# One encoder step: input and output projection in 7 Strassen products instead of 8, attention's data kept in device memory

## The chip, the cores and the metric

The kernel runs on one core of a Trainium2 chip. The metric is the device time of one execution in microseconds (us). A core has five engines with a program each: PE (TensorE, matrix products), DVE (VectorE), ACT (ScalarE), POOL (GpSimd) and SP, which here only issues transfers. They work side by side and wait for one another through semaphores. Operands lie in the on-chip buffer SBUF; PE writes its results into the accumulators PSUM, from which DVE and ACT take them in this kernel.

## The reference

One step of a hybrid encoder layer on 1056 tokens (a prompt of 1024 and a sample of 32), width 1024, everything in 32-bit floats:

```python
p = rmsnorm(x, g) @ w_in                       # 1024 -> 7424 columns
q, k, v, ga, bb, cc, hh, gb, xq, gx, mg = split(p)
attn  = window_attention(q, k, v, sink, alibi) # 8 heads, chunks of 64, 128 back
conv  = conv3(cc * hh, w, b)                   # 3 taps, each channel by itself
xattn = cross_attention(xq, mk, mv)            # 4 heads, 256 memory tokens, mk, mv = rmsnorm(mem) @ w
ya = (attn * silu(ga)) @ w_pa                  # 512 -> 1024
yb = (bb * conv * silu(gb)) @ w_pb
yx = (xattn * silu(gx)) @ w_px
sa, sb, sx = split(sigmoid(mg))
y = rmsnorm(x + (sa * ya + sb * yb + sx * yx) @ w_out, final_g)
```

The kernel also returns the new keys and values and the convolution's state.

## The kernel before

Activations lie with channels on the 128 partitions and tokens along the free dimension. Precision is kept by splitting each operand into a rounded high part and a rest (hi and lo, both in the type fp32r), and each product is three matmuls, hi·hi, hi·lo and lo·hi (`mm3`, L115 to L118). Tokens go in 3 chunks of 352.

x is loaded unnormalised, multiplied by the norm's gain and split once into `xhi` and `xlo` (`split_scaled`, L141). The input projection has 58 tiles of 128 output channels. Each tile and chunk is 8 pieces of the inner dimension times 3 matmuls of 352 columns into one PSUM bank, which DVE then multiplies by R, the reciprocal root mean square of each token (`scaled`, L285). Weights come as 172 pieces of 128x512 in the order of use: a load into `wraw`, a cast into `whi` on ACT (L102) and a subtraction into `wlo` on POOL (L103, the first 19 on DVE). They are made two or three pieces ahead of their use.

The order of the work is written out by hand: memory keys and values, k, v, q, then window attention and cross attention cut into steps that stand between the tiles of the other projections, the 24 tiles `mg` of the merge's gates in the middle, then the branch projections `y_tile` (matmuls of 352 columns) with the merge `z` (DVE L350 and POOL L662). `z` is split into `zhi` and `zlo` (L880). The output projection `wo` takes two forms: six blocks of 128 tokens with 512 columns, and the other 288 tokens with channels on the partitions (`wf`), turned by PE. One DVE instruction each adds the residual (L935), ACT sums the squares, POOL takes the power −0.5 and the result is scaled and stored block by block.

## Time and profile before

| | |
|---|---|
| three runs | 1050.56, 1051.35 and 1051.8 us, median 1051.35 us |
| the profiled execution | 1050.6 us span, as long as the fastest run |
| PE busy | 1033.7 us (98%) |
| DVE, ACT, POOL busy | 394.2, 338.7, 372.1 us |
| moved | 68.90 MB, 66 GB/s in the mean |

A busy time counts an engine's instructions with their overlaps taken out. For matmuls, which are pipelined, the spacing of the starts is the cost of one, and its own duration is longer. The chain of work that ended last says which engine the end waited for.

### The profile page before, as it was taken

Reading aid. Unit: us, or ns where it says so; the run is one execution under the profiler, and the core shown is the slowest. Engines: PE = TensorE matmul, PEld = TensorE weight load, DVE = VectorE, ACT = ScalarE, POOL = GpSimd, SP = SyncE. Lnnn points to the kernel's source line nnn. Section 1 sums busy time; section 2 is a strip of 40 time slices with the busy share of each in tenths; the row PEclk is TensorE's granted clock in tenths of the full one; section 3 lists DMA queues with packets and bytes.
Section 4 is the critical chain, followed back from the end, with each engine's and each line's share of the span. In section 5 each row is a group of like instructions: output and inputs, shape, how many; then the busy total and the mean of one; then the engine's idle time right before and its main releaser. Section 6 shows DMA issues by size and latency. Waiting matters only on the chain.

```text
span 1050.6 us, 16279 instructions
## 1 busy us (share of the span) xinstructions
PE 1033.7 (98%) x6531; PEld 1002.4 (95%) x6531; DVE 394.2 (38%) x747; ACT 338.7 (32%) x786; POOL 372.1 (35%) x353
## 2 busy tenths in 40 slices
PE   8999999999999999999999999999999999989997
PEld 7899999999999999999999999999999999988886
DVE  5736777773211244454111112222322111154122
ACT  7754555552121233344112111211212221233132
POOL 0353334241221232232333354434433453466210
PEclk9999999999999999999999999999999999999999
DMA  8861101011111111112111111111211221115112
GB/s 288 300 196 33 36 21 41 21 31 41 51 41 51 45 38 31 42 31 71 45 47 51 41 41 51 51 41 41 59 43 41 71 71 41 51 33 184 49 67 100
DMA packets 34827, 68.90 MB, mean 66 GB/s; under 512 B 4416, under 2 KB 5824, under 8 KB 34752
## 3 DMA queue, kind: packets, MB, share of 16 engines
q1 hardware_dynamic: 34752, 67.87, 20.5%
q8 instruction: 51, 0.84, 0.3%
q14 instruction: 24, 0.20, 0.1%
HBM read 62.31 MB, written 5.55 MB: 65 GB/s over the span
## 4 chain that ended last, share of the span: by engine, by line
PE 87%; DVE 7%; ACT 3%; issue 2%; DMA 1%; SPq 0%; DVEq 0%; POOLq 0%; POOL 0%; ACTq 0%
PE mg L116 8%; PE mg L117 8%; PE mg L118 8%; PE y L116 4%; PE y L117 4%; PE y L118 4%; PE wo L116 2%; PE wo L118 2%; PE wo L117 2%; PE gx L118 1%; PE gx L117 1%; PE xq L117 1%; PE xq L116 1%; PE xq L118 1%; PE gb L118 1%
## 5 line engine op out<-in xcount | busy, mean ns | idle before, releaser
L103 POOL TENSOR_TENSOR wlo<-wraw,whi 128x512 fp32r<-128x512 f32 x141 | 183.3, 1301 | 363.3 <-ACT whi L102 363.2
L102 ACT CAST whi<-wraw 128x512 fp32r<-128x512 f32 x160 | 99.0, 621 | 277.0 <-PE y L117 96.0
L116 PE MATMUL mg<-xhi,whi 128*128 128x352 f32 x576 | 186.6, 324 | 0.0
L117 PE MATMUL mg<-xlo,whi 128*128 128x352 f32 x576 | 185.8, 323 | 0.0
L118 PE MATMUL mg<-xhi,wlo 128*128 128x352 f32 x576 | 185.8, 323 | 0.0
L285 DVE TENSOR_TENSOR mg<-mg,R 128x352 f32<-128x352 f32 x72 | 38.3, 532 | 199.9 <-PE mg L118 199.7
L116 PEld LDWEIGHTS mg<-xhi,whi 128*128 128x128 f32 x576 | 108.2, 188 | 0.5
L117 PEld LDWEIGHTS mg<-xlo,whi 128*128 128x128 f32 x576 | 108.2, 188 | 0.0
L118 PEld LDWEIGHTS mg<-xhi,wlo 128*128 128x128 f32 x576 | 108.2, 188 | 0.0
L347 ACT ACTIVATE sg<-mg 128x352 f32<-128x352 f32 x51 | 23.7, 466 | 105.2 <-DVE mg L285 103.6
L662 POOL TENSOR_TENSOR z<-z,sg 128x352 f32<-128x352 f32 x42 | 39.7, 946 | 22.0 <-DVE sg L350 22.0
L350 DVE SCALAR_TENSOR_TENSOR sg<-sg,y 128x352 f32<-128x352 f32 x48 | 25.0, 520 | 59.2 <-PE y L118 46.6
L427 ACT ACTIVATE sw<-sw,mxw 128x256 f32<-128x256 f32 x64 | 31.8, 498 | 39.5 <-DVE mxw L444 39.4
L431 POOL TENSOR_TENSOR sw<-sw,rdw 128x1024 f32<-128x1024 f32 x16 | 30.3, 1896 | 29.7 <-DVE rdw L452 19.2
L116 PE MATMUL q<-xhi,whi 128*128 128x352 f32 x96 | 32.1, 334 | 0.0
L116 PE MATMUL y<-xqhi,whi 128*128 128x352 f32 x96 | 31.8, 331 | 0.0
L116 PE MATMUL ga<-xhi,whi 128*128 128x352 f32 x96 | 31.8, 331 | 0.0
L117 PE MATMUL y<-xqlo,whi 128*128 128x352 f32 x96 | 31.6, 329 | 0.0
L118 PE MATMUL y<-xqhi,wlo 128*128 128x352 f32 x96 | 31.5, 328 | 0.0
L116 PE MATMUL xq<-xhi,whi 128*128 128x352 f32 x96 | 31.2, 325 | 0.0
L116 PE MATMUL gx<-xhi,whi 128*128 128x352 f32 x96 | 31.2, 325 | 0.0
L117 PE MATMUL ga<-xlo,whi 128*128 128x352 f32 x96 | 31.1, 324 | 0.0
(354 smaller groups left out, 2770.8 us busy)
## 6 DMA issues: line engine op xcount, KB each, us to landing
wraw<-in_wst SPq DMA_DIRECT2D x172, 256.0 KB, 2.6
xsx<-in_x_prompt SPq DMA_DIRECT2D x8, 512.0 KB, 6.2
out_y_p<-y SPq DMA_DIRECT2D x7, 512.0 KB, 2.6
xp<-in_xT SPq DMA_DIRECT2D x6, 528.0 KB, 4.5
res<-in_x_prompt SPq DMA_DIRECT2D x8, 256.0 KB, 4.2
xp<-in_xT SPq DMA_DIRECT2D x3, 352.0 KB, 5.0
xsm<-in_mem_prompt SPq DMA_DIRECT2D x2, 512.0 KB, 5.2
x1z<-in_x_prompt SPq DMA_DIRECT2D x3, 256.0 KB, 6.9
```

Source lines behind the costliest of these rows:

```text
L102: act.copy(hi, raws[i])
L103: (eng or pool).tensor_tensor(out=lo, in0=raws[i], in1=hi.bitcast(F32), op=ALU.subtract)
L116: pe.matmul(out, lh, rh, start=first, stop=False)
L117: pe.matmul(out, lh, rl, start=False, stop=False)
L118: pe.matmul(out, ll, rh, start=False, stop=last)
L285: dve.tensor_tensor(out=ps, in0=ps, in1=R[:, ts], op=ALU.mult)
L347: act.activation(out, x, AF.Tanh, scale=0.5)
L350: dve.scalar_tensor_tensor(out=out, in0=t, scalar=1.0, in1=x, op0=ALU.add, op1=ALU.mult)
L427: act.activation(dst[:n, j, :w], src[:n, j, :w], AF.Exp, bias=nmx[:n, j:j + 1], scale=scale, accum_out=den[:n, j:j + 1])
L431: pool.tensor_tensor(out=s2v[:n, :cols, :w], in0=s2v[:n, :cols, :w], in1=rd[:n, :cols].unsqueeze(2).broadcast_to([n, cols, w]), op=ALU.mult)
L662: (pool if tail is None else dve).tensor_tensor(out=z, in0=z, in1=s[:, ts], op=ALU.add)
```

## The change

The tokens go in two halves c, of 528 tokens each, and each half again in two quarters of 264. For a pair of output tiles, the two halves of the inner dimension, the two output tiles and the two quarters of tokens make a 2x2 by 2x2 block product, which the Strassen-Winograd scheme does with 7 block products and sums of blocks (`group`). Both halves c are done with the same weights in the input projection, so that a group has 7 x 2 x 4 x 3 = 168 matmuls of 264 columns, where two tiles had 144 of 352.

For this x is normalised before it is used (`x_norm`), and the seven sums of its blocks are made and split (`x_combine`, 28 tiles). The weights need four sums of pieces on DVE per group (`Weights.comb`), and seven splits instead of four, with the subtraction on POOL unless a list names DVE. The seven results are put together with one copy or activation on ACT, a second one (`c11`), and five additions on DVE, each of a PSUM tile and an SBUF tile.

Since the 28 operand tiles fill the SBUF, q, k, v, the gates, the keys and values of the memory and the outputs of the branches are stored to device memory (`move`) and loaded back in pieces. Attention is cut into 51 units of four steps each, which are spread evenly over the products of the groups from `xq` on. The memory's keys and values are computed without a split, in plain fp32 matmuls. The output projection is done for one half c after the other: four groups each, of 84 matmuls, and the weights are combined and split again for the second half. It has channels on the partitions, and the result is stored transposed.

```diff
-        def split_scaled(raw, g, hi, lo):
-            act.activation(hi, raw, AF.Copy, scale=g)
-            dve.scalar_tensor_tensor(out=lo, in0=raw, scalar=g, in1=hi.bitcast(F32), op0=ALU.mult, op1=ALU.subtract)
...
-        def scaled(ps, ts):
-            dve.tensor_tensor(out=ps, in0=ps, in1=R[:, ts], op=ALU.mult)
-        def proj_chunk(w, c, evac, nm):
-            ps = pp.tile([128, CH], F32, name=f"{nm}_{c}", tag="pp")
-            ts = slice(c * CH, (c + 1) * CH)
-            for k in range(8):
-                wh, wl = w[k // 4]
-                cs = slice((k % 4) * 128, (k % 4 + 1) * 128)
-                mm3(ps, wh[:, cs], wl[:, cs], xhi[:, k, ts], xlo[:, k, ts], k == 0, k == 7)
-            evac(c, ts, ps)
...
-        def wo_token_major(half, i, c0, n_cols, ps):
-            ts = slice(i * 128, (i + 1) * 128)
-            for k in range(8):
-                wh, wl = splits[n_stream + half * 8 + k]
-                cs = slice(c0, c0 + n_cols)
-                mm3(ps, zhi[:, k, ts], zlo[:, k, ts], wh[:, cs], wl[:, cs], k == 0, k == 7)
...
-        def add_square(r, ps, n, acc, nm):
-            dve.scalar_tensor_tensor(out=r, in0=ps, scalar=0.5, in1=r, op0=ALU.mult, op1=ALU.add)
-            jk = wk.tile([128, 512], F32, name=f"jk{nm}", tag="pth", bufs=2)
-            act.activation(jk[:n, :r.shape[1]], r, AF.Square, accum_out=acc)
...
+        def move(out, in_):
+            out, in_ = (x.bitcast(F32) if x.dtype == F32R else x for x in (out, in_))
+            sp.dma_start(out=out, in_=in_)
...
+        def w_pair(src, name, eng=None):
+            n = src.shape[1]
+            hi = sb.tile([128, n], F32R, name=f"wh{name}", tag="whi", bufs=4)
+            lo = sb.tile([128, n], F32R, name=f"wl{name}", tag="wlo", bufs=4)
+            act.copy(hi, src)
+            sub_lo(eng or pool, lo, src, hi)
+            return hi, lo
...
+            def comb(self, i, a, b, op):
+                s = sb.tile([128, 512], F32, name=f"S{i}_{self.nm}", tag="S", bufs=3)
+                dve.tensor_tensor(out=s, in0=a, in1=b, op=op)
+                return s
+            def make(self, j):
+                self.load()
+                a11, a21, a22, a12 = self.raws
+                if j == 0:
+                    src = a11
+                elif j == 1:
+                    self.s1 = self.comb(1, a21, a22, ALU.add)
+                    src = self.s2 = self.comb(2, self.s1, a11, ALU.subtract)
+                elif j == 2:
+                    src = a12
+                elif j == 3:
+                    src = self.s1
+                elif j == 4:
+                    src = self.comb(3, a11, a21, ALU.subtract)
+                elif j == 5:
+                    src = self.comb(4, a12, self.s2, ALU.subtract)
                 else:
+                    src = a22
+                return w_pair(src, f"{self.nm}_{j}", self.engs[j])
...
+        def product(ps, cs, j, w, first, last):
+            for i, c in enumerate(cs):
+                for k in range(4):
+                    kc = slice(k * 128, (k + 1) * 128)
+                    mm3(ps[:, i, :H], w[0][:, kc], w[1][:, kc], XA[c][j][0][k], XA[c][j][1][k],
+                        first and k == 0, last and k == 3, True)
...
+            def s0():
+                st["a"], st["b"] = out_tile(0), out_tile(1)
+                st["pa"] = acc("pa", one_)
+                product(st["pa"], cs, B11, pair(), True, True)
+                act.copy(quad(st["a"], 0, cs), pv(st["pa"], cs))
+            def s1():
+                p = acc("pb", 1 - one_)
+                product(p, cs, T2, pair(), True, True)
+                st["u2"] = half("u2", f"u2{nm}")
+                dve.tensor_tensor(out=flat(st["u2"], cs), in0=pv(p, cs), in1=quad(st["a"], 0, cs), op=ALU.add)
+            def s2():
+                product(st["pa"], cs, B21, pair(), False, True)
+                c11(quad(st["a"], 0, cs), pv(st["pa"], cs))
+            def s3():
+                st["pc"] = acc("pc", 1 - one_)
+                product(st["pc"], cs, T1, pair(), True, True)
+                dve.tensor_tensor(out=quad(st["b"], 1, cs), in0=pv(st["pc"], cs), in1=flat(st["u2"], cs), op=ALU.add)
+            def s4():
+                st["pd"] = acc("pd", one_)
+                product(st["pd"], cs, T3, pair(), True, True)
+                q = quad(st["b"], 1, cs)
+                dve.tensor_tensor(out=q, in0=pv(st["pd"], cs), in1=q, op=ALU.add)
+            def s5():
+                product(st["pc"], cs, B22, pair(), False, True)
+                dve.tensor_tensor(out=quad(st["a"], 1, cs), in0=pv(st["pc"], cs), in1=flat(st["u2"], cs), op=ALU.add)
+                done(0, st["a"])
+            def s6():
+                product(st["pd"], cs, T4, pair(), False, True)
+                dve.tensor_tensor(out=quad(st["b"], 0, cs), in0=pv(st["pd"], cs), in1=flat(st["u2"], cs), op=ALU.add)
+                done(1, st["b"])
...
+            move(out=dst(0), in_=hi)
+            move(out=dst(1), in_=lo)
...
+        def x_norm(c, R):
+            for k in range(8):
+                dve.scalar_tensor_tensor(out=xk(c, k), in0=xk(c, k), scalar=cst[:, C_G + k:C_G + k + 1], in1=R,
+                                         op0=ALU.mult, op1=ALU.mult)
...
+            def put(op, kk, src):
+                hi, lo = (t[:, kk * 528:(kk + 1) * 528].rearrange("p (k h) -> p k h", k=2) for t in op)
+                act.copy(hi, src)
+                sub_lo((dve, pool, dve, pool, pool)[n[0] % 5], lo, src, hi)
+                n[0] += 1
...
+            def comb(out, a, b):
+                dve.tensor_tensor(out=out, in0=a, in1=b, op=ALU.subtract)
...
+            for kk in range(2):
+                put(b11, kk, xb(c, 0, 0, kk))
+            for kk in range(2):
+                t, u = (x[:, 2 * kk:2 * kk + 2] for x in tt)
+                comb(t, xb(c, 0, 1, kk), xb(c, 0, 0, kk))
+                comb(u, xb(c, 1, 1, kk), t)
+                put(t2, kk, u)
+                put(t1, kk, t)
+                t1s.append(u)
+                if kk == 0:
+                    b21 = operand(c, B21)
+                put(b21, kk, xb(c, 1, 0, kk))
...
+        def mv_step(k, w):
+            if k == 0:
                 for m in range(2):
+                    mps[m] = bank2(f"mvp{m}")[:, 0]
+            for m in range(2):
+                pe.matmul(mps[m], mt(k)[:, m * 128:(m + 1) * 128], w, start=k == 0, stop=k == 7)
...
+        units = win + [WindowSample()] + [Cross(h, u) for h in range(4) for u in range(4)] + [CrossSample(0), CrossSample(1)]
+        events = sorted((k + d, k, what) for k in range(len(units))
+                        for d, what in ((0.0, "load"), (1.0, "scores"), (2.5, "turn"), (3.02, "out")))
+        steps = [st for g in G[n_first:] for st in g]
+        end = events[-1][0] + 1
+        for i, st in enumerate(steps):
+            st()
+            while events and events[0][0] * (len(steps) - 4) <= i * end:
+                _, k, what = events.pop(0)
+                getattr(units[k], what)()
...
+        def z_put(c, j, p, src):
+            hi, lo = ZO[c, j][0][p], ZO[c, j][1][p]
+            act.copy(hi, src)
+            zn[0] += 1
+            sub_lo((dve, pool)[zn[0] % 2], lo, src, hi)
...
+        def z_second(c, p):
+            (z0, z1), (w0, w1) = z_pair(c, p), z_pair(c, 2 + p)
+            dve.tensor_tensor(out=z0, in0=w1, in1=z0, op=ALU.subtract)
+            z_put(c, T2, p, z0)
+            z_put(c, B21, p, w0)
+            pool.tensor_tensor(out=z1, in0=w1, in1=z1, op=ALU.subtract)
+            z_put(c, T3, p, z1)
+            z_put(c, B22, p, w1)
+            dve.tensor_tensor(out=w0, in0=w0, in1=z0, op=ALU.subtract)
+            z_put(c, T4, p, w0)
...
+            def done(i, r):
+                g = f + i
+                x = half("gt", f"xres{c}_{g}", F32, 3)
+                move(out=x, in_=A["xT"][c, g // 2][:, (g % 2) * 528:(g % 2 + 1) * 528])
+                dve.scalar_tensor_tensor(out=r, in0=r, scalar=0.5, in1=x, op0=ALU.mult, op1=ALU.add)
+                s = s2_tile(f"rsq{c}_{g}")
+                act.activation(s, r, AF.Square)
+                if g:
+                    pool.tensor_tensor(out=s, in0=s, in1=RT[c, "acc"], op=ALU.add)
+                RT[c, "acc"] = s
...
+        def finish(c):
+            R = r_chunk([RT[c, "acc"]], f"o{c}")
+            for g in range(8):
+                r = RT[c, g // 2 * 2][:, (g % 2) * 528:(g % 2 + 1) * 528]
+                fg = cst[:, C_FG + g:C_FG + g + 1]
+                if g % 3 == 2:
+                    act.activation(r, r, AF.Copy, scale=fg)
+                    pool.tensor_tensor(out=r, in0=r, in1=R, op=ALU.mult)
                 else:
+                    dve.scalar_tensor_tensor(out=r, in0=r, scalar=fg, in1=R, op0=ALU.mult, op1=ALU.mult)
+                move(out=O["yT"][c, g], in_=r)
```

Matmuls in the program, before and after, by columns: 352: 5040 and 0; 264: 0 and 6696; 512: 360 and 16 (the 16 in fp32); 288: 192 and 0; 256: 438 and 390, and 32 in fp32. Transposes go from 225 to 197. Other instructions: DVE 748 and 1082, ACT 656 and 836, POOL 350 and 471, transfers 244 and 569.

The first place is the start. POOL's queue of before, from the memory's keys (`mklo`) on; `wlo` are weights, `rsx` the powers that give R:

```order
L240 TENSOR_TENSOR mklo_95<-mstage_85,mkhi_94 128x256 x4
L103 TENSOR_TENSOR wlo19_461<-wraw19_428,whi19_460 128x512
L103 TENSOR_TENSOR wlo20_592<-wraw20_430,whi20_591 128x512
L103 TENSOR_TENSOR wlo21_596<-wraw21_464,whi21_595 128x512
L161 TENSOR_TENSOR rsx0_634<-vax0_632,cst_73 128x1
L161 TENSOR_TENSOR rsx1_643<-vax1_641,cst_73 128x1
L161 TENSOR_TENSOR rsx2_652<-vax2_650,cst_73 128x1
L161 TENSOR_TENSOR rsx3_693<-vax3_691,cst_73 128x1
```

And after, at the same place: `xl1_` are low parts of the operands of the second half, `mkl` those of the memory's keys, and `wlkv_1` belongs to the second product of the first group:

```order
L95 TENSOR_TENSOR xl1_3_457<-t11_458,xh1_3_456 128x528
L95 TENSOR_TENSOR mkl0_393<-mko0_389,mkh0_392 128x256
L95 TENSOR_TENSOR xl1_4_487<-xr1_0_128,xh1_4_486 128x528
L95 TENSOR_TENSOR xl1_3_457<-t11_458,xh1_3_456 128x528
L95 TENSOR_TENSOR wlkv_0_523<-rkv_0_514,whkv_0_522 128x512
L95 TENSOR_TENSOR mkl1_411<-mko1_407,mkh1_410 128x256
L95 TENSOR_TENSOR xl1_4_487<-xr1_1_130,xh1_4_486 128x528
L95 TENSOR_TENSOR xl1_5_493<-xr1_3_134,xh1_5_492 128x528
L95 TENSOR_TENSOR mkl2_429<-mko2_425,mkh2_428 128x256
L95 TENSOR_TENSOR xl1_6_499<-t21_459,xh1_6_498 128x528
L95 TENSOR_TENSOR wlkv_1_531<-S2_kv_528,whkv_1_530 128x512
L95 TENSOR_TENSOR wlkv_2_535<-rkv_3_520,whkv_2_534 128x512
```

POOL had one subtraction of weights after another there; now the low parts of x stand ahead of the first weights, and the second product's weights are row 37 of the queue.

The second place is the passage from the merge to the output projection. POOL before: `z5` is merged, then four tiles of z are split in one go, then come weights:

```order
L662 TENSOR_TENSOR z5_3037<-z5_3037,sg1_5_8615 128x352
L103 TENSOR_TENSOR wlo157_9000<-wraw157_8997,whi157_8999 128x512
L103 TENSOR_TENSOR wlo162_9116<-wraw162_9113,whi162_9115 128x512
L880 TENSOR_TENSOR zlo_8990<-z0_3036,zhi_8989 128x1056 x4
L103 TENSOR_TENSOR wlo163_9122<-wraw163_9119,whi163_9121 128x512
L103 TENSOR_TENSOR wl2_9126<-wraw164_9127,wh2_9125 128x512
L103 TENSOR_TENSOR wl2_9126<-wraw165_9131,wh2_9125 128x512
```

POOL after: `zo0_` and `zo1_` are operands of the halves 0 and 1, and `wlwo0c0_3` belongs to the fourth product of the first group of the output projection:

```order
L1007 TENSOR_TENSOR z0_1_10126<-z0_3_10370,z0_1_10126 128x2x264
L95 TENSOR_TENSOR zo0_2_1_10987<-z0_3_10370,zo0_2_0_10986 128x528
L95 TENSOR_TENSOR zo0_5_1_10991<-z0_3_10370,zo0_5_0_10990 128x528
L95 TENSOR_TENSOR zo1_1_1_11523<-z1_0_10015,zo1_1_0_11522 128x528
L1007 TENSOR_TENSOR z1_1_10153<-z1_3_10397,z1_1_10153 128x2x264
L95 TENSOR_TENSOR zo1_4_1_11527<-z1_0_10015,zo1_4_0_11526 128x528
L95 TENSOR_TENSOR zo1_2_1_11525<-z1_3_10397,zo1_2_0_11524 128x528
L95 TENSOR_TENSOR zo1_5_1_11529<-z1_3_10397,zo1_5_0_11528 128x528
L95 TENSOR_TENSOR wlwo0c0_3_11607<-S1_wo0c0_11572,whwo0c0_3_11606 128x512
L95 TENSOR_TENSOR zo1_6_1_11531<-z1_2_10275,zo1_6_0_11530 128x528
L95 TENSOR_TENSOR wlwo0c0_5_11647<-S4_wo0c0_11644,whwo0c0_5_11646 128x512
L95 TENSOR_TENSOR wlwo0c0_6_11665<-rwo0c0_2_11564,whwo0c0_6_11664 128x512
```

The weights of the fourth product now follow eight rows of z, some of them of half 1, which that group doesn't read.

The third place is the output projection. DVE before, for two and a half blocks of 128 tokens:

```order
L935 SCALAR_TENSOR_TENSOR res_9159<-wo0_0_9165,res_9159 128x512
L981 TENSOR_SCALAR ssq_9162<-ssq_9162 128x1
L935 SCALAR_TENSOR_TENSOR res_9159<-wo0_1_9196,res_9159 128x512
L981 TENSOR_SCALAR ssq_9162<-ssq_9162 128x1
L935 SCALAR_TENSOR_TENSOR res_9159<-wo0_2_9227,res_9159 128x512
```

DVE after, for one group of two tiles: `S1` to `S4` are sums of weights, `wl` low parts of them, `u2` and `res` the parts of the result:

```order
L131 TENSOR_TENSOR S4_wo2c0_11796<-rwo2c0_3_11590,S2_wo2c0_11705 128x512
L131 TENSOR_TENSOR S1_wo4c0_11856<-rwo4c0_1_11738,rwo4c0_2_11740 128x512
L95 TENSOR_TENSOR wlwo2c0_4_11779<-S3_wo2c0_11776,whwo2c0_4_11778 128x512
L212 TENSOR_TENSOR u2wo0_2_11774<-pbwo0_2_11757,res0_2_11730 128x264
L131 TENSOR_TENSOR S2_wo4c0_11858<-S1_wo4c0_11856,rwo4c0_0_11736 128x512
L131 TENSOR_TENSOR S3_wo4c0_11929<-rwo4c0_0_11736,rwo4c0_1_11738 128x512
L221 TENSOR_TENSOR res0_2_11730<-pcwo0_2_11795,u2wo0_2_11774 128x264
L227 TENSOR_TENSOR res0_2_11730<-pdwo0_2_11815,res0_2_11730 128x264
L95 TENSOR_TENSOR wlwo4c0_1_11861<-S2_wo4c0_11858,whwo4c0_1_11860 128x512
L231 TENSOR_TENSOR res0_2_11730<-pcwo0_2_11795,u2wo0_2_11774 128x264
L1043 SCALAR_TENSOR_TENSOR res0_2_11730<-res0_2_11730,xres0_2_11850 128x528
L236 TENSOR_TENSOR res0_2_11730<-pdwo0_2_11815,u2wo0_2_11774 128x264
```

Before, DVE had one long and one short instruction per block, each block 24 matmuls of 512 columns. Now it has twelve or thirteen long ones for each group of 84 matmuls, and eight of them read two tiles in SBUF.

## Rows read from the trace of the kernel before

**Rows 1.** The page: busy time, transfer rate in 40 slices, chain by engine.
```profile
PE 1033.7 (98%) x6531; PEld 1002.4 (95%) x6531; DVE 394.2 (38%) x747; ACT 338.7 (32%) x786; POOL 372.1 (35%) x353
...
GB/s 288 300 196 33 36 21 41 21 31 41 51 41 51 45 38 31 42 31 71 45 47 51 41 41 51 51 41 41 59 43 41 71 71 41 51 33 184 49 67 100
...
PE 87%; DVE 7%; ACT 3%; issue 2%; DMA 1%; SPq 0%; DVEq 0%; POOLq 0%; POOL 0%; ACTq 0%
```

**Rows 2.** Windows: stretch, length, each engine's busy time (instructions), clock, DMA share, GB/s.
```profile
0.00:50.00 50.00, 45.09 (x249) 39.55 (x250) 36.04 (x64) 37.69 (x75) 11.66 (x14) 1.00 0.84 288
50.00:100.00 50.00, 49.31 (x327) 46.76 (x327) 23.62 (x53) 26.03 (x65) 21.27 (x27) 1.00 0.43 138
100.00:200.00 100.00, 99.04 (x727) 95.34 (x726) 76.57 (x160) 53.35 (x168) 38.55 (x41) 1.00 0.10 30
...
950.00:1000.00 50.00, 49.99 (x275) 42.92 (x274) 11.24 (x21) 12.67 (x31) 21.66 (x17) 1.00 0.30 100
1000.00:1050.00 50.00, 44.03 (x246) 37.90 (x244) 14.73 (x30) 14.10 (x32) 5.36 (x9) 0.99 0.22 87
```

**Rows 3.** PE's timeline, 352 columns, first and last of ten; start, duration.
```profile
599.71 0.32 PE L116 MATMUL mg<-xhi,whi 128*128 128x352 f32 x1
...
601.15 0.32 PE L116 MATMUL mg<-xhi,whi 128*128 128x352 f32 x1
```

**Rows 4.** PE's timeline, 512 columns, first and last of ten.
```profile
950.83 0.40 PE L116 MATMUL wo<-woh,zhi 128*128 128x512 f32 x1
...
952.93 0.40 PE L116 MATMUL wo<-whi,zhi 128*128 128x512 f32 x1
```

**Rows 5.** PE's timeline, 288 columns, first and last of nine.
```profile
972.22 0.29 PE L117 MATMUL wf<-zlo,whi 128*128 128x288 f32 x1
...
973.28 0.29 PE L116 MATMUL wf<-zhi,whi 128*128 128x288 f32 x1
```

**Rows 6.** PE's timeline, 256 columns, first and last of 24.
```profile
1041.03 0.28 PE L116 MATMUL wo<-wh,zhi 128*128 128x256 f32 x1
...
1043.77 0.28 PE L118 MATMUL wo<-wh,zlo 128*128 128x256 f32 x1
```

**Rows 7.** DVE's timeline around the splitting of z.
```profile
934.15 2.25 DVE L662 TENSOR_TENSOR z<-z,sg 128x352 f32<-128x352 f32 x1
...
947.38 0.51 DVE L662 TENSOR_TENSOR z<-z,sg 128x352 f32<-128x352 f32 x1
...
949.87 1.07 DVE L662 TENSOR_TENSOR z<-z,sg 128x352 f32<-128x352 f32 x1
950.87 3.15 DVE L880 TENSOR_TENSOR zlo<-z,zhi 128x352 fp32r<-128x352 f32 x2
```

**Rows 8.** POOL's timeline around the splitting of z.
```profile
933.51 10.58 POOL L880 TENSOR_TENSOR zlo<-z,zhi 128x1056 fp32r<-128x1056 f32 x4 [0.95 <-ACT zhi L879]
...
949.01 9.93 POOL L103 TENSOR_TENSOR wl<-wraw,wh 128x512 fp32r<-128x512 f32 x7 [2.67 <-ACT wh L102]
```

**Rows 9.** POOL's line L103: minimum, median and maximum in ns.
```profile
L103 POOL TENSOR_TENSOR wlo<-wraw,whi x141: 1270/1289/2287, 38.8 to 944.1; 128x512 fp32r<-128x512 f32 x141
```

**Rows 10.** Groups by form: busy us, mean ns, idle before.
```profile
L103 DVE TENSOR_TENSOR wlo<-wraw,whi 128x512 fp32r<-128x512 f32 x19 | 12.7, 686 | 3.9 <-ACT whi L102 3.9
```

**Rows 11.** PE's timeline at the start: seven fp32 warm-up matmuls, then two of 512 columns.
```profile
1.45 3.35 PE L50 MATMUL wps<-warm 128*128 128x128 f32 x14 [1.45 <-DVE warm L46]
...
7.44 0.63 PE L116 MATMUL mvp<-whi,memt 128*128 128x512 f32 x1
7.86 0.63 PE L118 MATMUL mvp<-whi,memt 128*128 128x512 f32 x1
```

**Rows 12.** PE's timeline: the last matmul of the tile v.
```profile
60.16 0.33 PE L118 MATMUL v<-xhi,wlo 128*128 128x352 f32 x1
```

**Rows 13.** The page: the load of a weight piece, KB, us to landing.
```profile
wraw<-in_wst SPq DMA_DIRECT2D x172, 256.0 KB, 2.6
```

**Rows 14.** PE's timeline: the first matmul of the output projection.
```profile
945.70 0.50 PE L116 MATMUL wo<-whi,zhi 128*128 128x512 f32 x1 [3.58 <-DVE sg L350]
```

More of the change, by code (lines that the diff above doesn't have):

```diff
@@ new lines, in spread, with r_chunk @@
+        def spread(out, rs, j, w):
+            pe.matmul(out, rs[:w, j:j + 1].broadcast_to([w, 128]), ident[:w, :w], start=True, stop=True)
+        def r_chunk(parts, nm):
+            rs = column_rstd(parts, 6, 88, nm)
+            ps = bank2(f"rp{nm}")
+            for j in range(6):
+                spread(ps[:, j // 3, (j % 3) * 88:(j % 3 + 1) * 88], rs, j, 88)
+            r = half("u2", f"R{nm}")
+            act.copy(r.rearrange("p (s h) -> p s h", s=2), ps[:, :, :H])
+            return r
@@ L1004, in _tiles @@
+        for f in range(0, 8, 2):
+            for st in out_group(0, f):
+                st()
+        for f in range(0, 8, 2):
+            for st in out_group(1, f):
+                st()
+            if f == 0:
+                finish(0)
+        finish(1)
 def _tiles(w):
```

1463 lines of the change are left out of this document (674 added, 789 removed).

## The prediction

> **What bounds the kernel now.** The page says first who is busy: PE for 1033.7 of 1050.6 us, while DVE, ACT and POOL are each busy for about a third, and the chain that ended last is 87% PE [rows 1]. The table of stretches says where PE is not full: it loses 5 us in the first 50, 0.7 in the next, 1 between 100 and 200, nothing in the middle, and some 6 in the last 50 [rows 2]. So the time is PE's work plus two ends.
>
> What PE's work costs is read from start to start of neighbouring matmuls, not from their durations, which overlap. 352 columns take (601.15 − 599.71)/9 = 0.160 us [rows 3], 512 take 0.233 [rows 4], 288 take 0.1325 [rows 5], 256 take 2.74/23 = 0.119 [rows 6]. No row shows 264; on the line from 256 to 288 it is 0.122, in proportion to 352 it is 0.120. I take 0.122. By these the matmuls of before are 5040 × 0.160 + 360 × 0.233 + 192 × 0.133 + 438 × 0.119 = 968 us, and with transposes and small ones some 1011. The other 39 us are idle ends and some pipelining at the changes of tile.
>
> **A resource that the page doesn't list.** DVE multiplies two SBUF tiles of 128x352 in 0.51 us when POOL is idle (at 947.38), and the same instruction takes 2.25 at 934.15 [rows 7], while POOL subtracts its four tiles (933.51 to 944.09) [rows 8]. POOL pays too: one of its subtractions, 1.29 us in the median, took 2.29 [rows 9]. So an instruction of DVE with two SBUF inputs waits for the POOL instruction that runs, and then holds the next one up. For how long: seven subtractions took 9.93 us from 949.01 [rows 8], 7 × 1.29 = 9.03 alone; the 0.90 more are three DVE instructions of 352 that fell in that time (949.87, and two from 950.87) [rows 7], so 0.30 each, 0.21 less than such an instruction's length. One of 512 columns takes 0.69 [rows 10] and should hold POOL for 0.48. That is an estimate from two rows; its ends are 0 and the full 0.69.
>
> **The change, part by part**, against the profiled 1050.6 us, which is 0.8 under the median of the runs.
>
> 1. *PE's products.* 6696 × 0.122 + 390 × 0.119 = 863. The memory's plain fp32 products: seven of 128 columns took 3.35 us at the start, 0.48 each, so 1.9 for 512; but there fp32r products of 512 columns, too, start 0.42 apart [rows 11], against 0.233 later, so later it is some 0.95 to 1. I take 16 × 0.9 + 32 × 0.45 = 29. With the small ones 935 in all: **−77** (−90 at 0.120 and with fp32 at the speed of fp32r, −70 with fp32 dearer).
>
> 2. *The start.* Before, PE could begin on a raw chunk; v's last matmul starts at 60.16 [rows 12], and up to there some 49 us of the listed work were done, so 11 were idle. Now the first group needs normalised, combined and split operands of both halves. The first R needs half of x (2.16 MB, 7.5 us at 288 GB/s [rows 1]), squares, their sum and its spreading: about 20 us. Then POOL has, until the second product's weights, 22 subtractions and additions of 512 or 528 columns at 1.30, three of half that and the powers: 32 us. DVE has 50 instructions with two SBUF inputs, 50 × 0.48 = 24 of POOL's time. One after the other: 20 + 56 = 76. Six more products of 24 × 0.122 = 2.9 follow: the group ends at 94, with 54 us of work done, so 40 idle: **+30**. If DVE held POOL up for nothing, it would end at 70 (+5); with slower stats 42.
>
> 3. *Groups with window attention* (twelve of them, from `xq` to `bg`, and some `mg`). PE has 168 × 0.122 + 3.6 of attention = 24.1 us per group. DVE's list, with 0.69 for 512 columns [rows 10] and less in proportion for fewer, is 17 to 21 us, POOL's at 1.3 each [rows 9] 12 to 17. Of DVE's, 8 to 12 read two SBUF tiles and wait for a POOL instruction, 0.3 to 0.5 us on average: 21 to 25 us. Before, DVE had 77 us in such a 100 and PE stayed at 99% [rows 2]. I take 1 us per group lost: **+12** (0 to 40). The spills lie beside: a piece of 256 KB lands in 2.6 us [rows 13], and 20 to 70 GB/s were moved here, out of 300 shown [rows 1]. Groups of `mg` with cross attention have 11 to 14 us on DVE, and cost nothing.
>
> 4. *The branch projections* wait for the first branch's 4.3 MB, 15 us at 288 GB/s, whose places come free with the last groups' operands: some 17 us of products still cover it. **+4** (0 to 10).
>
> 5. *From the merge to the output projection.* Before, PE stood for 3.58 us [rows 14]. Now POOL's subtraction for the fourth product stands behind eight rows of z (10.4 us), and DVE's 16 instructions on two SBUF tiles hold it up by 7.7. Four more weights (5.2) and the group ends about 24 us after the merge's last product, with 10.25 of work: 14 idle, **+10** (0 to 20).
>
> 6. *The output groups.* 84 × 0.122 = 10.25 us of PE each. POOL has five subtractions and two additions of squares, 7 × 1.30 = 9.1; DVE has eight instructions on two SBUF tiles, 8 × 0.48 = 3.8. Together 12.9. ACT has seven casts and four more instructions, each shorter than one of POOL's, and is not the bound. Seven groups lose 2.65 each, 18.5, and the first half's finish falls between (5.5); what POOL has made ahead takes some back: **+20** (0 to 32).
>
> 7. *The end.* Before, the last matmul starts at 1043.77 [rows 6], which leaves 6.6 us after its end. Now it is an addition, a residual, a square, the sum on POOL (2.9), column sums, power, spreading and copy (3.2), eight tiles scaled (4.6) and stored (3): 14. **+7** (+3 to +9).
>
> Sum: −77 + 30 + 12 + 4 + 10 + 20 + 7 = +6, so 1057. The ends together are 975 and 1134, but they don't all come at once.
>
> **The rivals.**
>
> *A, faster: DVE slips in beside POOL.* The hold of 0.48 rests on three instructions, of 352 columns. What hangs on it: 50 instructions in the start, 16 in the passage, 8 × 7 in the output groups, 122 in all, 58 us at 0.48. With none the time is about 1000, with half 1028; I put it at 1018. Against it stands the POOL instruction that took 2.29 [rows 9]. The point from which it decides is near: 6/122 = 0.05, so a hold of 0.43 already makes the change even.
>
> *B, slower: DVE becomes the bound under window attention.* If the waits for POOL come at 0.8 us instead of 0.4, as with the 2.25 us of [rows 7], each of the twelve groups takes 28 us instead of 25: +36, 1093. For it speaks that all seven evacuations go through DVE or ACT in order, so a late one holds a PSUM pair that the next product needs; against it, the 99% of before.
>
> *C, slower: DVE holds POOL up for its whole length,* 0.69 and not 0.48: 122 × 0.21 = +26, 1083. The rows give the lower value, if the POOL durations in them can be trusted to 0.2 us. The Trainium skill's page "SBUF — State Buffer", section "SBUF: two separate sides", states this rule: the port pair that DVE and GpSimd share is an exclusive lock, held for the whole instruction, and a DVE instruction with two SBUF inputs takes it; the trace agrees that they exclude each other, but its 0.90 us for three is less than the rule's 1.5.
>
> *D: seven products aren't cheaper.* If 264 columns cost what 288 do, PE's work is 74 more, 1131. The rows on both sides speak against it.
>
> **How the numbers follow.** Forecast 0.40 (1035 to 1080, of both signs: 0.15 faster, 0.04 same, 0.21 slower), A 0.27 (0.26 faster, 0.01 same), B 0.18, C 0.12, D 0.03. A difference of 0.2% (2 us) is about what a measurement of this kernel can tell from no change. Faster 0.41, same 0.05, slower 0.54. The range 1010 to 1110 leaves out about a quarter of A, a fifth of B and D: 0.14.
>
> **What would show it.** Step 1: starts of 264 columns 0.122 apart, and a sum of PE's spacings near 935. Step 2: the `kv` group's last matmul at 94; before 80, the waits on POOL are overrated there. Step 3: the groups `ch` at 24 to 26 us each, PE waiting for DVE. Step 5: 14 us idle in front of the first `wo` products, POOL as the releaser. Step 6: groups of the output projection every 12 to 13 us, with POOL full; 10.3 us would refute it. Step 7: 14 us from the last matmul to the end. The prediction fails if DVE's long instructions are not seen beside POOL's, or if transfers, which I count at nearly nothing, hold the attention units up.

## The result, and the profile after

The changed kernel takes 1139.21 us (median of four runs, 1138.41 to 1139.88) where the kernel before took 1051.57 in the runs beside it: a ratio of 1.0837, with an interval of 1.0822 to 1.0852. I had forecast 1057 and a range up to 1110.

The page of the changed kernel, whose profiled execution spans 1137.8 us, to be held against [rows 1]:

```profile
PE 1008.9 (89%) x7743; PEld 975.2 (86%) x7743; DVE 658.0 (58%) x1081; ACT 436.7 (38%) x936; POOL 586.7 (52%) x470
...
PE   4678999999997998897999999999989997688774
...
PEclk9698999999998999899999999999999999888877
...
GB/s 343 21 120 134 193 142 125 135 165 132 126 70 109 70 101 78 99 78 90 138 135 166 145 191 149 147 146 144 271 350 214 213 124 95 0 104 112 114 104 77
...
PE 43%; DVE 13%; POOL 6%; issue 4%; ACT 2%; DMA 2%; DVEq 0%; POOLq 0%; ACTq 0%
```

PE's busy time did fall, but it fills 89% of the span where it filled 98%. DVE's busy time has grown by 264 us and POOL's by 215, and of the chain that ended last PE has 43% of the span. That chain was followed back only to 331.5 us, so its shares add up to 70%: PE has some 61% of what was followed, where it had 87% of the whole span. The row of the clock is mostly 9s in the middle and has 6 to 8 at both ends, where the row of PE is low too.

Windows of the same trace (columns as in [rows 2]) show where PE is not full:

```profile
0.00:50.00 50.00, 23.78 (x88) 17.25 (x89) 25.49 (x33) 22.06 (x40) 19.87 (x16) 0.87 0.54 196
50.00:110.00 60.00, 49.82 (x265) 42.51 (x265) 43.48 (x43) 24.17 (x43) 40.47 (x30) 0.85 0.40 122
110.00:193.00 83.00, 83.00 (x683) 82.95 (x682) 40.16 (x53) 31.46 (x53) 36.69 (x28) 1.00 0.48 148
193.00:520.00 327.00, 303.39 (x2407) 293.03 (x2406) 227.59 (x447) 141.13 (x345) 167.78 (x154) 0.96 0.36 108
520.00:822.00 302.00, 296.18 (x2438) 292.89 (x2437) 148.95 (x305) 136.60 (x311) 140.40 (x121) 1.00 0.50 156
822.00:980.00 158.00, 144.91 (x1153) 143.25 (x1152) 59.47 (x73) 24.66 (x40) 78.25 (x57) 0.98 0.54 185
980.00:1117.00 137.00, 103.41 (x698) 99.38 (x697) 104.91 (x119) 54.75 (x102) 95.89 (x62) 0.83 0.29 90
1117.00:1137.00 20.00, 4.43 (x28) 3.90 (x27) 7.90 (x10) 1.88 (x3) 7.34 (x5) 0.64 0.29 109
```

These stretches are the stages: the start up to the end of the group `kv`; the groups `q` and `ga`, which have no attention beside them and are full; the twelve groups with window attention; `mg` with cross attention; the branch projections; the output projection; the end. By them the forecast and the measurement are:

| stage | forecast, us | measured, us |
|---|---|---|
| start to the end of `kv` | 94 | 110 |
| `q`, `ga` | 82 | 83 |
| groups with attention, `xq` to `mg` | 606 | 629 |
| branch projections | 144 | 158 |
| output projection, with the passage to it | 116 | 137 |
| end | 14 | 20 |

(The 116 are 82 of products, the 14 idle of step 5 and the 20 of step 6; the forecast's 606 is what is left of its 1057 after the others.) Everything that runs without attention and without a change of stage came out to 1 us. The miss of 81 us is spread over all the rest.

What a row of it looks like is seen in the output projection. DVE's timeline of the changed kernel (start, duration, instruction, idle before):

```profile
1011.27 0.69 DVE L131 TENSOR_TENSOR S_wo2c<-rwo2c,S_wo2c 128x512 f32<-128x512 f32 x1
...
1012.60 1.83 DVE L95 TENSOR_TENSOR wlwo2c<-S_wo2c,whwo2c 128x512 fp32r<-128x512 f32 x1
1014.35 0.42 DVE L212 TENSOR_TENSOR u2wo<-pbwo,res 128x264 f32<-128x264 f32 x1
...
1016.06 1.77 DVE L131 TENSOR_TENSOR S_wo4c<-rwo4c,rwo4c 128x512 f32<-128x512 f32 x1
1017.75 0.42 DVE L221 TENSOR_TENSOR res<-pcwo,u2wo 128x264 f32<-128x264 f32 x1
```

and POOL's in the same stretch:

```profile
1013.84 1.75 POOL L95 TENSOR_TENSOR wlwo2c<-S_wo2c,whwo2c 128x512 fp32r<-128x512 f32 x1
1015.55 1.74 POOL L95 TENSOR_TENSOR wlwo2c<-rwo2c,whwo2c 128x512 fp32r<-128x512 f32 x1
1017.24 1.73 POOL L95 TENSOR_TENSOR wlwo4c<-rwo4c,whwo4c 128x512 fp32r<-128x512 f32 x1
```

The subtraction `wl` on DVE takes 1.83 us, the sum `S` 1.77, each for work that takes 0.69 when POOL is quiet (1011.27, and [rows 10]). Instructions that read PSUM for one input keep their 0.42. POOL's subtractions take 1.74 instead of 1.29 [rows 9]. So while both have work here, they take turns, an instruction each, and neither goes at its own pace. The 0.45 us by which POOL's instruction is longer is the hold that the prediction put at 0.48.

PE's part in this is a wait and something behind it:

```profile
1032.40 0.36 PE L99 MATMUL pcwo<-zo,whwo4c 128*128 128x264 f32 x1 [2.33 <-DVE res L221]
...
1034.05 0.42 PE L99 MATMUL pdwo<-zo,whwo4c 128*128 128x264 f32 x1
...
1036.47 0.42 PE L101 MATMUL pdwo<-zo,wlwo4c 128*128 128x264 f32 x1
```

PE stands for 2.33 us in front of `pcwo` until DVE's addition `res` is done, runs on, and from 1034.05 to 1036.47 twelve matmuls take (1036.47 − 1034.05)/11 = 0.22 us each, nearly twice the 0.1225 that 264 columns take elsewhere (1016.26 to 1016.75, four intervals, in the same trace). The window of these twelve has a granted clock of 0.50:

```profile
1034.05:1036.47 2.42, 2.42 (x12) 2.42 (x12) 1.14 (x2) 1.26 (x2) 1.66 (x1) 0.50 0.64 212
```

That is the lower of the engine's two clock levels, 1.2 instead of 2.4 GHz; in the whole output stage it is 0.83, against 1.00 in `q` and `ga`. In all, the trace has 18 stretches of 5 to 25 such matmuls, 247 of them, which lose about 0.10 us each, 26 us. The forecast had nothing for it.

### The profile page after: what moved, and what is told of

It is laid out like the page before. It is cut to its first block, busy times and chain, and to the rows that moved or that the text cites. A ratio compares the mean times of both kernels' runs of the same rounds, so it can differ in the third digit from the quotient of the medians.

```text
span 1137.8 us, 20296 instructions
## 1 busy us (share of the span) xinstructions
PE 1008.9 (89%) x7743; PEld 975.2 (86%) x7743; DVE 658.0 (58%) x1081; ACT 436.7 (38%) x936; POOL 586.7 (52%) x470
## 4 chain that ended last, share of the span: by engine, by line
PE 43%; DVE 13%; POOL 6%; issue 4%; ACT 2%; DMA 2%; DVEq 0%; POOLq 0%; ACTq 0%
PE y L99 3%; PE y L100 3%; PE y L101 3%; PE pcmg L99 2%; PE pdmg L99 2%; PE pcmg L101 2%; PE pdmg L101 2%; PE pcmg L100 2%; PE pdmg L100 2%; PE pamg L99 2%; PE pamg L101 2%; PE pamg L100 2%; DVE och L300 1%; DVE zo L95 1%; DVE res L1060 1%
## 5 line engine op out<-in xcount | busy, mean ns | idle before, releaser
L95 POOL TENSOR_TENSOR wlmg<-S_mg,whmg 128x512 fp32r<-128x512 f32 x48 | 62.0, 1292 | 64.1 <-ACT whmg L115 59.3
L99 PE MATMUL pamg<-xh,whmg 128*128 128x264 f32 x192 | 55.3, 288 | 3.3 <-ACT omg L206 3.3
L99 PE MATMUL pcmg<-xh,whmg 128*128 128x264 f32 x192 | 55.5, 289 | 0.3 <-DVE omg L221 0.3
L99 PE MATMUL pdmg<-xh,whmg 128*128 128x264 f32 x192 | 55.1, 287 | 0.0
L101 PE MATMUL pamg<-xh,wlmg 128*128 128x264 f32 x192 | 54.6, 284 | 0.0
L101 PE MATMUL pcmg<-xh,wlmg 128*128 128x264 f32 x192 | 54.6, 284 | 0.0
L100 PE MATMUL pamg<-xl,whmg 128*128 128x264 f32 x192 | 54.6, 284 | 0.0
L101 PE MATMUL pdmg<-xh,wlmg 128*128 128x264 f32 x192 | 54.5, 284 | 0.0
L100 PE MATMUL pcmg<-xl,whmg 128*128 128x264 f32 x192 | 54.5, 284 | 0.0
L100 PE MATMUL pdmg<-xl,whmg 128*128 128x264 f32 x192 | 54.4, 283 | 0.0
```

The source lines that it names most:

```text
L95: eng.tensor_tensor(out=lo, in0=x, in1=hi.bitcast(F32), op=ALU.subtract)
L99: pe.matmul(out, lh, rh, start=first, stop=False, skip_group_check=free)
L100: pe.matmul(out, lh, rl, start=False, stop=False, skip_group_check=free)
L101: pe.matmul(out, ll, rh, start=False, stop=last, skip_group_check=free)
```

## The experiments

The theory after the result (theory 1): DVE and POOL exclude each other, and what is spread over both to share the work costs more than on DVE alone. The rival (theory 2): DVE has too much to do, and moving anything to it makes it worse. They part where POOL's work is given to DVE. Theory 1 holds two things that these edits change together: the waits of each engine for the other, and POOL's own pace, 1.29 us for a subtraction that DVE does in 0.69.

**Moving the subtractions of weights, stage by stage.** In the output projection:

```diff
-                            [pool, dve, pool, pool, dve, pool, pool])
+                            [dve] * 7)
```

> Edit: in the output projection all seven subtractions of weights of a group go to DVE (before: two on DVE, five on POOL). Theory 1 (DVE and POOL exclude each other: a DVE instruction with two SBUF inputs waits for the running POOL instruction, 1.77 us instead of 0.69): the groups of the output projection, 13.5 to 17 us each now, take 11 to 12.5, the stage 20 us less, the kernel about 1119 us. Theory 2 (DVE simply has too much to do): its list grows by 5 x 0.62 = 3.1 us per group, the stage by up to 25, the kernel about 1164 us.

Measured: 1117.45 us (ratio to before 1.0631, 1.0615 to 1.0647), 22 us less than the changed kernel. In the twelve groups with window attention:

```diff
-            add(f"ch{f}", T_CC + f, T_HH + f, conv_in_group(f))
+            add(f"ch{f}", T_CC + f, T_HH + f, conv_in_group(f), [dve] * 7)
...
```

(and the same for `xq`, `gx` and `bg`.)

> Edit: the subtractions of weights of the twelve groups with window attention (xq, gx, ch, bg) go from POOL to DVE. Theory 1 (mutual exclusion): the groups, 27.3 us on average now, take 25 to 25.5, the kernel about 1115 us. Theory 2 (DVE's own work is the bound there): its list grows by 7 x 0.62 = 4.3 us per group, the groups take 31 us, the kernel about 1185 us. Theory 3 (the chain through one attention unit is too long for the steps it is given, whoever subtracts): no change beyond 0.5%, 1139 us.

Measured: 1115.66 us (1.0610, 1.0594 to 1.0626), 24 us less. The stage of the twelve groups in the trace of this kernel:

```profile
193.00:495.00 302.00, 294.15 (x2400) 285.57 (x2399) 257.83 (x528) 141.46 (x344) 64.89 (x73) 0.99 0.38 116
```

It takes 302 us instead of 327. DVE is busy for 258 of them, more than the 228 of before the edit, POOL for 65 instead of 168, and PE waits less. Theory 2 is out, since DVE got more work and the stage got shorter, and so is theory 3 of the expectation. How much of it is the waiting of DVE can be read from its 48 sums of weights in this stage (line L131), in the changed kernel, in this one, and in the kernel with nearly nothing on POOL (below):

```profile
193.00:520.00 327.00, 49.22 (x48) 0.96 0.36 108
...
193.00:495.00 302.00, 37.15 (x48) 0.99 0.38 116
...
191.00:484.00 293.00, 32.54 (x48) 1.00 0.39 121
```

They take 1.03, 0.77 and 0.68 us on average. So the edit took 12 us of waiting from them, and 25 from the stage. At the start:

```diff
-                sub_lo((dve, pool, dve, pool, pool)[n[0] % 5], lo, src, hi)
+                sub_lo(dve, lo, src, hi)
```

> Edit: at the start the low parts of x's operands are all made on DVE (before: 12 of 28 on DVE, 16 on POOL). Theory 1 (mutual exclusion): the first group, which ends at 110 us now, ends at 95 to 98, the kernel about 1126 us. Theory 2 (DVE's work is the bound): 16 x 0.65 = 10 us later, the kernel about 1149 us.

Measured: 1141.88 us (1.0857, 1.0841 to 1.0873), no gain at all; the first group ends at 110.9. Taking these instructions from POOL changes nothing here by itself, and both theories failed. All three edits, the rest of the weights and z's splitting:

```diff
-            sub_lo(eng or pool, lo, src, hi)
+            sub_lo(eng or dve, lo, src, hi)
...
-            sub_lo((dve, pool)[zn[0] % 2], lo, src, hi)
+            sub_lo(dve, lo, src, hi)
```

> Edit: every subtraction that makes low parts of weights, of x and of z goes to DVE, in all stages (POOL keeps the memory's low parts, the softmax products, the merge's additions and the squares' additions). Theory 1 (mutual exclusion): the gains of the three single edits and a few us in the passage to the output projection add up: about 1075 us. Theory 2 (DVE's work is the bound): their losses add up, above 1200 us.

Measured: 1082.02 us (1.0296, 1.0278 to 1.0313). The gains of the first two (22 and 24 us) add up, and 11 us more come for the most part from the branch projections, whose weights are now split on DVE too: 150 us instead of 158 in the traces.

**Going on with it.** On top of that kernel, nearly all other long instructions of POOL go to DVE; two of the edits:

```diff
-            pool.tensor_tensor(out=s2v[:n, :cols, :w], in0=s2v[:n, :cols, :w],
+            dve.tensor_tensor(out=s2v[:n, :cols, :w], in0=s2v[:n, :cols, :w],
...
-                    (dve if last else pool).tensor_tensor(out=zv, in0=zv, in1=sv, op=ALU.add)
+                    dve.tensor_tensor(out=zv, in0=zv, in1=sv, op=ALU.add)
```

> Edit, on top of the kernel with all subtractions on DVE (1082 us): nearly everything else that POOL did on long tiles goes to DVE as well (softmax products, the merge's and squares' additions, the conv branch's products, z's differences, the memory's low parts). Theory 1 (mutual exclusion still costs): another 5 to 10 us less, about 1075 us. Theory 2 (DVE, already 87 to 89% busy under window attention, is now the bound by its own work): 10 to 15 us more, about 1095 us.

Measured: 1057.65 us (1.0059, 1.0040 to 1.0077), 24 us less, more than expected. The stages of the twelve groups and of the output projection here:

```profile
191.00:484.00 293.00, 292.70 (x2409) 284.97 (x2408) 263.53 (x567) 142.64 (x346) 12.15 (x34) 1.00 0.39 121
924.00:1034.00 110.00, 93.23 (x699) 90.06 (x698) 102.01 (x179) 53.98 (x102) 6.54 (x3) 0.94 0.36 112
```

DVE is busy for 264 of 293 us, POOL for 12, and PE for 292.7: it has no wait left there. Under attention a DVE at 90% does not hold PE up, a DVE at 70% beside a POOL at 51% did. In the output stage it is otherwise: DVE is busy for 102 of 110 us, PE for 93, and PE's longest wait there is for a subtraction on DVE (us in total, times, longest):

```profile
PE pcwo L101 <- DVE wlwo0c L95: 7.6, 1, 7.6
```

So once POOL is out of that stage, DVE's own list holds PE up.

**The unit's own chain.** On the kernel with all subtractions on DVE, the last step of an attention unit is put later:

```diff
-                        for d, what in ((0.0, "load"), (1.0, "scores"), (2.5, "turn"), (3.02, "out")))
+                        for d, what in ((0.0, "load"), (1.0, "scores"), (2.5, "turn"), (3.5, "out")))
```

> Edit, on top of the kernel with all subtractions on DVE (1082 us): the last step of each attention unit comes 0.48 of a unit's time later (some 5 us of PE). If PE's waits under window attention that are left (6 us before ow, and the slower clock behind them) are the unit's own chain: 8 us less, about 1074 us. If DVE's whole list is the bound there, the wait only moves to the next evacuation: no change, 1080 to 1083 us.

Measured: 1076.99 us (1.0244, 1.0228 to 1.0259), 5 us less, between the two. The waits before `ow` were a chain that came late, and without POOL in it (above) 0.3 us of them is left without this edit.

**Undoing one part: the output projection by plain products.** On the same kernel; the additions of squares go from POOL to DVE with it. The core of the new tile:

```diff
+            for s in range(2):
+                for k in range(8):
+                    kc = slice((k % 4) * 128, (k % 4 + 1) * 128)
+                    hs = slice(s * H, (s + 1) * H)
+                    mm3(ps[:, s, :H], w[k // 4][0][:, kc], w[k // 4][1][:, kc], ZH[c, k][0][:, hs], ZH[c, k][1][:, hs],
+                        k == 0, k == 7)
```

> Edit, on top of the kernel with all subtractions on DVE (1082 us): the output projection is done by plain products again, 16 tiles of 48 matmuls of 264 columns (768 instead of 672), with no sums of weights or of z. Theory 1 (DVE and POOL, not PE, set the pace of the output stage): the stage takes its matmuls' 768 x 0.1215 = 93 us instead of 111, the passage before it some 5 us less, the kernel about 1060 us. Rival (the seven products are worth their saving there): 96 x 0.1215 = 12 us more, about 1094 us.

Measured: 1061.88 us (1.0098, 1.0073 to 1.0123), 20 us less. The window of the stage:

```profile
940.00:1041.00 101.00, 99.31 (x795) 98.83 (x793) 51.11 (x76) 35.05 (x57) 5.35 (x3) 0.97 0.37 120
```

It takes 101 us with 768 matmuls (expected 93), where it took 111 with 672 (137 in the changed kernel), and PE is full: in this stage the seven products cost more in sums and splits than they save on PE. With nearly nothing on POOL the same step is worth less, 9 us (1042.54 to 1033.23, between two of the kernels below).

**The start.** A kernel on the same base leaves out seven eighths of the products for the memory's keys and values:

```diff
-        for k in range(8):
+        for k in range(1):
             mv_step(k, wmv[k])
...
-            for k in range(8):
+            for k in range(1):
                 cs = slice((k % 4) * 128, (k % 4 + 1) * 128)
-                pe.matmul(ps, w[k // 4][:, cs], mt(k), start=k == 0, stop=k == 7)
+                pe.matmul(ps, w[k // 4][:, cs], mt(k), start=True, stop=True)
```

> Edit, on top of the kernel with all subtractions on DVE (1082 us): of the memory's keys and values only the first of eight pieces of the inner dimension is computed (48 fp32 matmuls become 6), all else stays; a count of PE's time, since the memory's products are left out. If PE's fp32 products in front of the first group are what makes it late: the group ends at 95 to 97 instead of 109, the kernel about 1069 us. If it is the chain of statistics, normalising and combining on ACT, POOL and DVE: 106 to 109 us, the kernel 1079 to 1082.

Measured: 1079.93 us in one run; the first group begins at 59.5 instead of 75.7 and ends at 107.2 instead of 108.9. So PE's fp32 products account for 2 us of it and are not what makes it late. The trace of the kernel with x's low parts all on DVE says what is. POOL there:

```profile
43.63 6.13 POOL L369 TENSOR_TENSOR rsx<-vax,cst 88x6 f32<-88x6 f32 x1 [5.72 <-DVE vam L366]
49.74 0.69 POOL L369 TENSOR_TENSOR rsm<-vam,cst 128x2 f32<-128x2 f32 x1
```

ACT:

```profile
50.46 0.69 ACT L516 ACTIVATE mvo<-mvp,rsm 128x512 f32<-128x512 f32 x1 [12.34 <-POOL rsm L369]
...
52.71 0.60 ACT L382 COPY Rx<-rpx 128x528 f32<-128x528 f32 x1 [0.92 <-PE rpx L373]
...
53.90 0.64 ACT L435 CAST xh<-t 128x528 fp32r<-128x528 f32 x1
```

and DVE:

```profile
43.39 0.16 DVE L366 TENSOR_SCALAR vax<-csx 88x6 f32<-88x6 f32 x1 [8.69 <-PE csx L362]
...
55.63 0.71 DVE L95 TENSOR_TENSOR xl<-t,xh 128x528 fp32r<-128x528 f32 x1 [7.07 <-ACT xh L435]
...
61.82 2.80 DVE L417 SCALAR_TENSOR_TENSOR xr<-xr,cst,Rx 128x528 f32<-128x528 f32 x4
```

DVE's queue holds a small instruction (`vax`) that needs the second half's column sums, and has stood 8.69 us for it when that runs at 43.39. Then POOL's power `rsx`, 88x6, takes 6.13 us instead of 1.33 (at 19.31 in the same trace), since DVE runs eight instructions with two SBUF inputs in a row from 43.54 to 48.6; ACT stands for 12.34 us behind the next power, `rsm`, with x's casts queued behind; DVE stands for 7.07 us behind those casts; and the second half is normalised only from 61.82. The second half's statistics are late, because its data come behind 3.1 MB of loads for the memory. So it was put first, on the kernel with nearly nothing on POOL, where these powers start at 43.68 and 49.79; the two additions of the second half's squares on POOL go to DVE with it. The core of the edit:

```diff
         x_load(0, [slot(1, j, l) for j in (B21, T3) for l in range(2)])
+        x_load(1, [slot(1, j, l) for j in (B22, T4) for l in range(2)])
...
-        x_load(1, [slot(1, j, l) for j in (B22, T4) for l in range(2)])
...
         R0 = x_stats(0)
+        R1 = x_stats(1)
         for i in range(4):
             mem_scale(i)
-        R1 = x_stats(1)
```

> Edit, on top of the kernel with nearly nothing on POOL (1058 us): the second half of x is loaded right after the first, ahead of the memory's 3.1 MB, and its squares are summed ahead of the memory's. If the first group is late because the second half's reciprocal root comes late (its power ends at 49.8 us, DVE is idle for 8.4 and 7.1 us around it): it ends 12 to 15 us sooner, at 93 to 96 instead of 108, the kernel about 1044 us. If the amount of normalising, combining and splitting on DVE and ACT is the bound: 105 to 108, the kernel 1055 to 1058.

Measured: 1042.54 us (0.9916, 0.9897 to 0.9936), 15 us less, and 0.8% under the kernel before. POOL's powers there:

```profile
36.35 1.34 POOL L369 TENSOR_TENSOR rsx<-vax,cst 88x6 f32<-88x6 f32 x1 [5.89 <-DVE vax L366]
37.67 0.78 POOL L369 TENSOR_TENSOR rsm<-vam,cst 128x2 f32<-128x2 f32 x1
```

They end at 38.5 instead of 50.5, each in its own time. The first group's last matmuls, in the changed kernel and in this one (ns least, median, most; first and last start in us):

```profile
L101 PE MATMUL pdkv<-xh,wlkv x16: 278/286/289, 101.4 to 109.8; 128*128 128x264 f32 x16
...
L101 PE MATMUL pdkv<-xh,wlkv x16: 278/284/289, 88.2 to 96.6; 128*128 128x264 f32 x16
```

The group ends at 96.9 instead of 107.9 in the kernel that the edit was put on, so 11 of the 15 us are the start (12 to 15 were expected); the rest is spread over the later stages. The same edit on the changed kernel itself:

> Edit, on the changed kernel itself: only the second half of x first, ahead of the memory's loads, its squares summed on DVE ahead of the memory's. If the late second half is what made the start miss its 94 us, POOL's and DVE's exclusion apart: the first group ends 12 to 15 us sooner than 110, the kernel at 1125 us. If with 16 subtractions on POOL the exclusion takes its place (77 us of both in a row from 20 us on): the first group at 100 to 106, the kernel 1130 to 1135.

Measured: 1129.99 us (1.0745, 1.0727 to 1.0763), 9 us less; the first group ends at 102.4. There the late half and POOL's work share the start: 8 us and 5.5 us (102.4 against 96.9) of the 16 by which it missed the forecast. That the edit on x's low parts alone showed nothing fits this: the late half covered it.

**All that helped, together**: nearly nothing on POOL, plain products at the output, the second half of x first.

> Edit: the edits that helped, together: nearly nothing on POOL, the output projection by plain products, the second half of x first. By adding up: 1058 - 13 for the output stage (110 to 97 us) - 13 for the start = about 1030 us, 2% under the kernel before; if the gains share one cover, 1040 to 1045.

Measured: 1033.23 us (0.9824, 0.9807 to 0.9841), 1.8% under the kernel before and near the 1030 of adding up. Its page:

```profile
PE 981.6 (95%) x7827; PEld 956.9 (93%) x7827; DVE 728.3 (71%) x1370; ACT 415.6 (40%) x884; POOL 34.8 (3%) x58
...
PE   3969999999999999999999999999998999999994
...
PEclk9989999999999999999999999999999999999897
```

## Why the prediction was wrong, by its steps

*Step 1 was right in its prices and too hopeful in its sum.* 264 columns take 0.1225 us, as read off the neighbours, and the stages without attention take what the count of matmuls says (83 us for four groups). Rival D falls with it. But PE's work was to fall by some 77 us, from 1011 to 935, and the pages have 1033.7 and 1008.9; 26 of the latter is the slow pace told above, so at the full clock it fell by some 51. In the last kernel it is some 69 (981.6, less 12 for its 96 additional matmuls and 5 of slow pace). The memory's fp32 products take 0.86 us for 512 columns at the full clock (two passes of 0.43), as estimated.

*The mechanism was right and its price was not: steps 3, 5 and 6, and part of 4.* The prediction found the exclusion in two rows and priced it, in steps 5 and 6, as POOL's time alone: so many DVE instructions, 0.48 us each. That hold was 0.45. What these steps left out is the other side: an instruction of DVE that meets a busy POOL takes 1.77 us instead of 0.69, 1.1 more. The mean durations by group in the trace of the changed kernel (busy us, mean ns, idle before) are far above the 0.69 to 0.75 that they have alone, but for the last one, which reads PSUM:

```profile
L95 DVE TENSOR_TENSOR zo<-z,zo 128x528 fp32r<-128x528 f32 x14 | 18.4, 1338 | 0.3
...
L417 DVE SCALAR_TENSOR_TENSOR xr<-xr,cst,Rx 128x528 f32<-128x528 f32 x16 | 16.4, 1084 | 5.0 <-ACT Rx L382 5.0
...
L131 DVE TENSOR_TENSOR S_bg<-rbg,rbg 128x512 f32<-128x512 f32 x8 | 11.5, 1438 | 1.9 <-POOL wlch L95 1.8
L253 DVE SCALAR_TENSOR_TENSOR z<-s,y 128x528 f32<-128x528 f32 x16 | 11.2, 704 | 40.5 <-PE y L101 32.7 <-DMA s<-MGd 7.8
```

Step 3 did count that side, at 0.3 to 0.5 us on average, and the average was right: the 48 sums of weights there take 1.03 us, 0.34 more than alone, with `S_bg` at 1.44 the worst. What failed in it is the 1 us lost per group: a group takes 327/12 = 27.3 us, 3.2 more than PE's 24.1. It was summed as if the engines' totals decided, and they didn't: DVE was busy for 228 of 327 us and POOL for 168. Where PE stands there, a chain through queues that run in order comes late. Its longest wait, 4.3 us in front of `ow` at 353.33, leads back through ACT to two products on POOL:

```profile
PE ow L99 <- ACT pthw L555: 7.6, 2, 4.3
...
349.92 0.64 ACT L263 ACTIVATE ehcb<-gb 128x528 fp32r<-128x528 f32 x1 [3.65 <-POOL gb L322]
...
348.25 3.35 POOL L322 TENSOR_TENSOR gb<-gb,och 128x528 f32<-128x528 f32 x2 [1.49 <-DVE gb L253]
```

ACT, with the cast that PE needs behind it in its queue, stands 3.65 us for the first `gb`, which waits for DVE, and DVE has waited for a subtraction on POOL. The two products take 3.35 us, and 2.6 if each took the least of its line, 1.32. So the exclusion is some 0.7 us of this wait, and the order in the queues and POOL's own pace are the larger part as far as these rows show. How the 34 us by which the stage is longer than with POOL out of it (327 against 293) divide between these causes is not shown: every edit that takes work from POOL removes them together.

With POOL out of it, the twelve groups take 293 us instead of 327 (forecast 301), the branch projections 145 instead of 158 (144), the output projection 110 instead of 137 (116). In the first two the forecast is met once POOL is gone. In the output projection it is met by luck: the 116 held 34 us put down mainly to POOL, and in the 110, with POOL busy for 6.5, the longest wait is for DVE's own work.

*A price that was missing: the clock.* Behind most of its longer waits PE went on at 0.22 us per matmul, for 1 to 6 us; not behind all, the 3.3 us before 530.25 were followed by no such stretch. It is 26 us of the changed kernel by the count above, 14 of them in the output projection, and 5 us in the last kernel, which has few waits. Against it stand some 117 us of gaps in the changed kernel and 37 in the last one, so a wait of PE cost its own length and about a fifth on top.

*Step 2 failed for another reason.* I had the second half's operands limited by POOL's and DVE's time, 76 us by then. They were limited by the order of loads and by what stood in front in in-order queues: the runs with x's low parts on DVE (no gain) and with the second half first (the group ends 11 us sooner) show it. One long wait is left inside the first group even in the last kernel: PE stands 10.2 us for the first weights' low part, `wlkv` on DVE.

*Step 7 was too short by 6 us.* The rows of the end, of the changed kernel, on POOL, PE, DVE and SP:

```profile
1118.14 3.07 POOL L1047 TENSOR_TENSOR rsq<-rsq,rsq 128x528 f32<-128x528 f32 x2 [2.45 <-ACT rsq L1045]
...
1124.03 2.86 PE L373 MATMUL rpo<-cst,rso 88*128 88x88 f32 x12 [1.66 <-POOL rso L369]
...
1127.56 6.34 DVE L1060 SCALAR_TENSOR_TENSOR res<-res,cst,Ro 128x528 f32<-128x528 f32 x6 [5.00 <-ACT Ro L382]
...
1128.92 5.51 SPq L49 DMA_DIRECT2D out_yT<-res  x8
```

Two additions on POOL, one behind the other, take 3.07 us where I had one; the spreading is in fp32 and takes 2.86; six scalings take 6.34 beside POOL's, where 6 x 0.70 = 4.2 would do.

*The rivals.* A (DVE slips in beside POOL) is refuted by the rows of 1.7 us and by the runs that took work from POOL under attention and at the output. C (a hold of the full 0.69) is refuted by the 0.45. The Trainium skill's page "SBUF — State Buffer", section "SBUF: two separate sides", says of the port pair that whoever starts first has it for the whole instruction and the other fully blocks; the trace agrees that the other blocks, while the time that an instruction of DVE adds to one of POOL is 0.24 us less than its length. B named a stage that did lose, and its price was nearly right (28 us per group; 27.3 measured), but not its reason: its waits of 0.8 us are 0.34 on average in the 48 sums, and DVE was not full and grew fuller as the kernel grew faster. That its price came out is luck. The spill, counted at nearly nothing, stayed so where the trace shows it: no wait of PE under attention names a transfer. At the beginning of the branch projections DVE stands 7.8 us for the gates that come back from device memory behind the first branch (the last of the groups above), and PE 3.6 us for DVE: step 4 had 4, though it thought of the branch's own data. The measured time also lies above both ends that the prediction gave for its sum, 975 and 1134 (the lower is 969 by its own terms): start, branch projections and end each lost more than the most that their steps allowed, 42, 10 and 9 us more than in the kernel before.

What stays open: how much the seven products bring in the input projection by themselves, since no run has plain products there, and how much of POOL's price is exclusion and how much its slower instructions.

## What to carry to other kernels

A second engine that shares the work is not free capacity when it is slower at it and the two exclude each other: compare one instruction's duration with its neighbour busy and idle, and price the wait on both sides, in the chain as well as in the totals. A trade that saves time on a full engine by giving work to half-empty ones is to be checked stage by stage for chains that run through two queues, and each wait of PE is to be priced with the slow matmuls behind it. Where a stage begins, look at what stands first in the load queue and in the in-order queues: 3.1 MB for later use cost 11 us here.
